# Delta-rule mixer: the identity added while evicting, projection products in threes, the last gate's products tied to the scan

## The chip, the cores and the metric

The kernel runs on one core of a Trainium2 chip. Its time is device time in microseconds, from one launch to its end; the time before is the median of three runs. The engines are TensorE (PE in the profile, with its weight loads as PEld), VectorE (DVE), ScalarE (ACT), GpSimd (POOL, idle here) and SyncE (SP), which issues the transfers. Each engine works through its own instructions in the order in which they were built.

## The reference, cut to what matters

Two network blocks run one after the other on 256 tokens of width 1024. The second holds, as its first mixer, a gated delta rule with 8 heads of 128 channels. Per head the tokens (256 of context and 256 of the sequence, in both directions) are cut into chunks, a triangular system is solved in each chunk, and a state is carried from chunk to chunk:

```python
lower = jnp.where(strict, jnp.einsum('nhcid,nhcjd->nhcij', kb, k) * decay, 0.0)
uw = lax.linalg.triangular_solve(lower, rhs, left_side=True, lower=True, unit_diagonal=True)
...
v_new = u_c - jnp.einsum('nhik,nhkv->nhiv', w_c, state)
o = jnp.einsum('nhik,nhkv->nhiv', qg_c, state) + jnp.einsum('nhij,nhjv->nhiv', qk_c, v_new)
state = state * a_c[..., None, None] + jnp.einsum('nhjk,nhjv->nhkv', kd_c, v_new)
```

q, k, v and a gate z come from projections of the modulated tokens; the outputs of the heads are normalised, gated by silu(z) and projected back.

## The kernel before

**Products.** A projection runs at fp32 accuracy as three products of split operands: with a high and a low part of each, `mm3` adds high by high (L172), low by high (L173) and high by low (L174) into one PSUM bank. One projection of 128 output channels on 512 tokens has 8 slices of the inner dimension and so 24 products of 128x512; in the trace they are `proj<-xh,whi`, `proj<-xl,whi` and `proj<-xh,wlo`. A head needs four such projections: q, k and v (through `dn_conv`, with a convolution over five taps, L964 and the lines next to it, on VectorE) and the gate z, at the end of `dn_scan`. The weights come by DMA in 512 KB pieces and are split on ScalarE (`whi`) and VectorE (`wlo`).

**The inverse.** `dn_inverse` inverts the triangular matrices of one head. There are two units, one per direction, each of four 128x128 matrices. Five levels are worked through, two units each, so a head has 10 steps and the stage 80. With the inverse x so far, its transpose xt and the level's mask m, a step is: `pw` = four f16 products of m and xt; w = pw copied to f16 by ScalarE (L1016); `pt` = identity times xt, one 128x512 product (L991), and four products of x and w added onto it; the new xt copied from `pt` by ScalarE (L1020); `px` = four products of w and x; the new x = x + px, added by VectorE (L1024). The tiles `dn_pw`, `dn_pt`, `dn_px` and `dn_pr` share two PSUM banks (tag `inv`). Each step of the one unit begins when a bank is free, and so the 10 steps follow each other: `dn_pw` starts a step, and the next `dn_pw` waits for the eviction of `dn_pt`. A closing part after the ten steps (64-wide products, a transpose, one refinement with fp32 products `dn_pr`, L1052 and L1055) gives the fp32 inverse `dn_xf`.

**The scan.** `dn_scan` carries the state through four chunks in two directions with fp32 products of 128x128 (`dn_st`, `dn_ob`, L1152 to L1171) and small evictions, then takes the gate's projection, normalises and writes y. After the last head the out-projection starts, with the same three products per slice; its tiles are named `proj` and `dn_pr`.

**What sets the order.** The code is written in the order solve(0), then for each head solve(head+1) and scan(head). A scheduler of the framework builds each engine's instruction list from this: among the instructions that it takes to be ready it places the one with the lowest priority number, which by default counts up in the order of the code. So the products of a later projection stand between the products of a step as filler: one, two or three of them while TensorE waits for w or for xt. `issue_after` is a means of that framework that holds instructions behind a named one, if it is on the same engine.

Of the kernel before, what the change touches and what calls it, by code (L numbers as in the profile page):

```python
# [14 lines left out]
AF = mybir.ActivationFunctionType  # L15
ALU = mybir.AluOpType
# [5 lines left out]
KD = D // P  # L22
S = 256
F = 2816
KF = F // P
EPS = 1e-6
WARM = 16


# [74 lines left out]
class Kernel:  # L104
# [60 lines left out]
            los.append(lo)  # L165
        return Split(his, n, shape), Split(los, n, shape)

    def mm3(self, out, pairs, first=True, last=True):

        n = len(pairs)  # L170
        for i, ((ah, al), (bh, bl)) in enumerate(pairs):
            self.nc.tensor.matmul(out, ah, bh, start=first and i == 0, stop=False)  # L172
            self.nc.tensor.matmul(out, ah, bl, start=False, stop=False)  # L173
            self.nc.tensor.matmul(out, al, bh, start=False, stop=last and i == n - 1)  # L174


    def rsqrt(self, out, x, shape, tag=""):
# [690 lines left out]

        self.nc.tensor.transpose(out, col.to_broadcast((P, P)), self.ident)

    def project2(self, w, j, x, name="proj2"):

        wh, wl = self.weight(w[j])
        m = wh.shape[2]
        flat = lambda t: t.rearrange("p s t -> p (s t)")
        ps = self.ch.psum([P, 2, S], name)
        self.mm3(flat(ps[:m]), [((wh[:, k], wl[:, k]), (flat(x[0][:, k]), flat(x[1][:, k]))) for k in range(KD)])
        return ps

    def project_apart(self, jobs, x, between=lambda: None):  # L880
# [94 lines left out]
    def dn_inverse(self, units):  # L975
# [3 lines left out]
        V, G = nc.vector, nc.scalar  # L979
        i16 = self.ident16.unsqueeze(1).to_broadcast((P, 4, P))  # L980
# [8 lines left out]
        def each(out, lhs, rhs, more=None):  # L989
            if more is not None:  # L990
                nc.tensor.matmul(out, self.ident16, more, start=True, stop=True)  # L991
            for c in range(4):
                nc.tensor.matmul(out[:, c], lhs[:, c], rhs[:, c], start=more is None, stop=True, skip_group_check=more is not None)  # L993
# [9 lines left out]
        xs, xts = [], []  # L1003
# [5 lines left out]
        for lv in range(1, 6):  # L1009
            ms = [off(n, lv) for n in range(2)]  # L1010
            for n in range(2):
                x, xt = xs[n], xts[n]
                pw = ch.psum([P, 4, P], "dn_pw")
                each(pw, ms[n], xt)
                w = new("dn_wm", 2)
                G.activation(w, pw, AF.Copy)  # L1016
                pt = ch.psum([P, 4, P], "dn_pt")
                each(pt, x, w, xt)
                xts[n] = new("dn_xt")
                G.activation(xts[n], pt, AF.Copy)  # L1020
                px = ch.psum([P, 4, P], "dn_px")
                each(px, w, x)
                xs[n] = new("dn_x")
                V.tensor_tensor(xs[n], x, px, op=ALU.add)  # L1024

        ws = []
        for n in range(2):
# [104 lines left out]
    def dn_scan(self, h, x, gt, parts, y):  # L1132
# [10 lines left out]
        for n in range(4):  # L1143
            if n % 2 == 0:
                ob = ch.psum([P, 2, P], "dn_ob")
            for d in range(2):
                s, c = st[d], n ^ d
                ps = ch.psum([P, 4, P], "dn_st")
                if s is None:
                    rhs = vt[:, c]  # L1150
                else:
                    nc.tensor.matmul(ps[:, 0], k[:, c], s, start=True, stop=True)  # L1152
                    rhs = ch.loc([P, P], "dn_rr", bufs=2)
                    V.scalar_tensor_tensor(rhs, ps[:, 0], at("neg", d, c), vt[:, c], op0=ALU.mult, op1=ALU.add)
                nc.tensor.matmul(ps[:, 1], xi[d][:, c], rhs, start=True, stop=True)
                if n < 3:
                    vk = ch.loc([P, P], "dn_vk", bufs=2)
                    G.activation(vk, ps[:, 1], AF.Copy, scale=at("bk", d, c))
                vn = ch.loc([P, P], "dn_vn", bufs=2)
                G.activation(vn, ps[:, 1], AF.Copy, scale=at("beta", d, c))  # L1160
                if n < 3:
                    nc.tensor.matmul(ps[:, 3], kt[:, c], vk, start=True, stop=True)
                    s2 = ch.loc([P, P], "dn_s", bufs=4)
                    if s is None:
                        V.tensor_copy(s2, ps[:, 3])
                    else:
                        V.scalar_tensor_tensor(s2, s, at("ge", d, c), ps[:, 3], op0=ALU.mult, op1=ALU.add)
                    st[d] = s2
                if s is not None:
                    nc.tensor.matmul(ps[:, 2], q[:, c], s, start=True, stop=True)  # L1170
                nc.tensor.matmul(ob[:, c % 2], dms[d][:, c], vn, start=n % 2 == 0 and d == 0, stop=n % 2 == 1, skip_group_check=True)  # L1171
                if n in (1, 2):
                    G.activation(o[:, c], ps[:, 2], AF.Copy, scale=at("eg", d, c))
                elif n == 3:
                    V.scalar_tensor_tensor(o[:, c], ps[:, 2], at("eg", d, c), o[:, c], op0=ALU.mult, op1=ALU.add)
            if n % 2:
                V.tensor_tensor(o[:, n - 1:n + 1], o[:, n - 1:n + 1], ob, op=ALU.add)
        pz = self.project2(self.A["dn_w"], 24 + h, x)
        z = ch.loc([P, 2, S], "dn_z", bufs=2)
        G.activation(z, pz, AF.Tanh, scale=0.5)  # L1180
        V.scalar_tensor_tensor(z, z, 1.0, pz, op0=ALU.add, op1=ALU.mult)
# [496 lines left out]
```

## Time and profile before

| | |
|---|---|
| time, median of three runs | 3092.65 us (3091.64 to 3095.69) |
| the profiled execution, its own time | 3096.87 us |
| its span, first to last instruction | 3095.1 us |
| mean granted TensorE clock | 0.987 of full speed (2.4 GHz) |
| TensorE busy | 3028.9 us, 98% |
| VectorE busy | 2383.8 us, 77% |
| ScalarE busy | 1846.0 us, 60% |
| delta-rule stage with the 80 steps, first to last `dn_pw` | 1557.84 to 1921.83 us |

The page gives the busy time of each engine over the span, then the span in 40 slices, the transfers, the chain of work that ended last, and the costliest groups. A matmul row's duration (0.39 us for most) is its latency; TensorE starts the next one before it ends, so what an instruction costs TensorE is the distance from its start to the next start. A busy TensorE can therefore still hold small waits.

### The profile page before, as it was taken

To read this page: it belongs to the slowest core of one execution; us is meant where nothing else is said; L and a number is where in the kernel's file an instruction comes from. 1 tells how busy PE (TensorE), PEld (TensorE's weight loads), DVE (VectorE), ACT (ScalarE), POOL (GpSimd) and SP (SyncE) were. 2 spreads that over 40 slices of the span, in tenths; PEclk is the share of its full clock that TensorE was granted. 3 is DMA by queue.
4 is the path that set the end of the run, shared out by engine and by line. 5 is a ranking of instruction groups with operands and counts; after the bars stand their busy time and mean duration, and the time that the engine had idled before them with its cause. 6 is when DMAs were issued, how large, how long until landed. Compare 5 with 4: busy or idle time off the path is not lost.

```text
span 3095.1 us, 53671 instructions
## 1 busy us (share of the span) xinstructions
PE 3028.9 (98%) x19974; PEld 2672.8 (86%) x19974; DVE 2383.8 (77%) x5017; ACT 1846.0 (60%) x3803; POOL 0.2 (0%) x4
## 2 busy tenths in 40 slices
PE   9999999999999999999999999999999999998999
PEld 9998999999899988888777777888888888896999
DVE  7888887888878878777888888677776766677766
ACT  5656566556665656666587777456554555556555
POOL 0000000000000000000000000000000000000000
PEclk9999999999999999999999999999999999998999
DMA  7653565566356635555211111244553444440455
GB/s 241 217 167 98 177 202 178 175 193 211 105 160 189 206 120 170 163 176 172 88 39 36 42 48 35 96 147 157 161 174 110 138 143 146 143 131 34 137 180 169
DMA packets 129861, 438.90 MB, mean 142 GB/s; under 512 B 14528, under 2 KB 18368, under 8 KB 129088
## 3 DMA queue, kind: packets, MB, share of 16 engines
q1 hardware_dynamic: 129456, 435.22, 44.3%
q8 instruction: 157, 2.57, 0.3%
q14 instruction: 104, 0.85, 0.1%
q10 hardware_dynamic: 144, 0.26, 0.0%
HBM read 433.32 MB, written 1.05 MB: 140 GB/s over the span
## 4 chain that ended last, share of the span: by engine, by line
PE 89%; DVE 5%; ACT 3%; DMA 1%; issue 1%; SPq 0%; ACTq 0%; DVEq 0%
PE gu L173 15%; PE gu L172 15%; PE gu L174 15%; PE dn L174 7%; PE dn L172 7%; PE dn L173 7%; PE proj L172 4%; PE proj L173 4%; PE proj L174 4%; DVE wlo L147 1%; ACT whi L146 1%; PE dn_pw L993 1%; PE dn_px L993 1%; PE dn_pt L993 1%; PE swa_pt L1347 1%
## 5 line engine op out<-in xcount | busy, mean ns | idle before, releaser
L146 ACT ACTIVATE whi<-raw 128x512 fp32r<-128x512 f32 (+1 forms) x1398 | 835.9, 604 | 860.4 <-PE gu L173 427.1
L147 DVE TENSOR_TENSOR wlo<-raw,whi 128x512 fp32r<-128x512 f32 (+1 forms) x1398 | 907.6, 657 | 407.7 <-ACT whi L146 393.8
L172 PE MATMUL gu<-xh,whi 128*128 128x256 f32 (+1 forms) x2800 | 907.3, 324 | 8.2 <-ACT xh L316 2.2
L173 PE MATMUL gu<-xl,whi 128*128 128x256 f32 (+1 forms) x2800 | 906.7, 324 | 0.9 <-DVE xl L325 0.7
L174 PE MATMUL gu<-xh,wlo 128*128 128x256 f32 (+1 forms) x2800 | 905.2, 324 | 0.2 <-DVE wlo L147 0.2
L172 PEld LDWEIGHTS gu<-xh,whi 128*128 128x128 f32 x2800 | 531.1, 190 | 54.2 <-ACT xh L324 4.4
L173 PEld LDWEIGHTS gu<-xl,whi 128*128 128x128 f32 x2800 | 530.9, 190 | 46.6 <-DVE xl L325 1.7
L174 PEld LDWEIGHTS gu<-xh,wlo 128*128 128x128 f32 x2800 | 530.4, 190 | 45.0 <-DVE wlo L147 0.4
L172 PE MATMUL dn<-hh,whi 128*128 128x256 f32 (+1 forms) x1388 | 447.4, 324 | 0.8
L174 PE MATMUL dn<-hh,wlo 128*128 128x256 f32 (+1 forms) x1388 | 446.5, 323 | 1.2 <-DVE wlo L147 1.2
L173 PE MATMUL dn<-hl,whi 128*128 128x256 f32 (+1 forms) x1388 | 446.0, 322 | 0.0
L172 PE MATMUL proj<-xh,whi 128*128 128x256 f32 (+2 forms) x936 | 307.6, 331 | 11.5 <-ACT lora_raw L542 4.0
L174 PE MATMUL proj<-xh,wlo 128*128 128x256 f32 (+2 forms) x936 | 307.1, 330 | 4.1 <-DVE wlo L147 4.1
L173 PE MATMUL proj<-xl,whi 128*128 128x256 f32 (+2 forms) x936 | 307.9, 331 | 2.1 <-DVE xl L317 1.9
L172 PEld LDWEIGHTS dn<-hh,whi 128*128 128x128 f32 x1388 | 263.1, 190 | 27.3 <-ACT hh L146 4.5
L174 PEld LDWEIGHTS dn<-hh,wlo 128*128 128x128 f32 x1388 | 262.7, 190 | 25.2 <-DVE wlo L147 3.9
L173 PEld LDWEIGHTS dn<-hl,whi 128*128 128x128 f32 x1388 | 263.4, 190 | 23.9 <-DVE hl L147 2.4
L172 PEld LDWEIGHTS proj<-xh,whi 128*128 128x128 f32 (+1 forms) x936 | 177.3, 190 | 22.0 <-ACT lora_raw L542 4.2
L174 PEld LDWEIGHTS proj<-xh,wlo 128*128 128x128 f32 (+1 forms) x936 | 177.9, 190 | 13.6 <-DVE wlo L147 4.9
L173 PEld LDWEIGHTS proj<-xl,whi 128*128 128x128 f32 (+1 forms) x936 | 177.8, 190 | 11.3 <-DVE xl L317 3.3
L461 DVE TENSOR_TENSOR ada_t<-ada_w,ada_c 128x1024 f32<-128x1024 f32 x144 | 175.4, 1218 | 6.2 <-DMA ada_w<-in_ada_w 6.2
L461 DVE TENSOR_TENSOR ada_w<-ada_w,ada_c 128x1024 f32<-128x1024 f32 x144 | 175.4, 1218 | 0.6
(522 smaller groups left out, 4016.6 us busy)
## 6 DMA issues: line engine op xcount, KB each, us to landing
raw<-in_ffn_gate SPq DMA_DIRECT2D x176, 512.0 KB, 3.8
raw<-in_ffn_up SPq DMA_DIRECT2D x176, 512.0 KB, 3.6
ada_w<-in_ada_w SPq DMA_DIRECT2D x144, 512.0 KB, 3.8
raw<-in_ffn_down SPq DMA_DIRECT2D x80, 448.0 KB, 3.4
raw<-in_ffn_down SPq DMA_DIRECT2D x40, 512.0 KB, 4.0
raw<-in_ffn_down SPq DMA_DIRECT2D x48, 384.0 KB, 3.2
raw<-in_dn_w SPq DMA_DIRECT2D x32, 512.0 KB, 3.4
raw<-in_ffn_down SPq DMA_DIRECT2D x48, 320.0 KB, 3.0
```

Source lines behind the costliest of these rows:

```text
L146: self.nc.scalar.activation(hi, src, AF.Copy)
L147: return self.nc.vector.tensor_tensor(lo, src, hi.bitcast(F32), op=ALU.subtract)
L172: self.nc.tensor.matmul(out, ah, bh, start=first and i == 0, stop=False)
L173: self.nc.tensor.matmul(out, ah, bl, start=False, stop=False)
L174: self.nc.tensor.matmul(out, al, bh, start=False, stop=last and i == n - 1)
L461: V.tensor_tensor(p, w, c[:, s], op=ALU.mult)
L993: nc.tensor.matmul(out[:, c], lhs[:, c], rhs[:, c], start=more is None, stop=True, skip_group_check=more is not None)
L1347: self.pinned(nc.tensor.transpose(pt[:, k], p[:, k // 2, (k % 2) * P:(k % 2 + 1) * P], self.ident))
```

## The change

Three things are changed.

1. In a step of the inverse, the eviction of `pw` goes from ScalarE to VectorE and adds the identity: w' = pw + I. Since x w' = x w + x, in either product, the transposed inverse is then `pt` = x w' without the product of the identity and xt, and the new x is `px` = w' x without the addition. The eviction of `px` goes from VectorE to ScalarE as a plain copy. 80 products of 128x512 go; the number of evictions stays.
2. `mm3` gets a switch `together`. With it, the second and third product of a slice get a priority number a million lower, so that the scheduler places them right behind the first. `project2` (q, k, v and z of each head, and not the out-projection, which calls `mm3` itself) sets it, except for the gate of head 7.
3. The gate of head 7 is wrapped in `issue_after(begun.ins)`, where `begun` is the ScalarE activation that writes `vn` in the first chunk of the last scan. That is an instruction of ScalarE, the products are TensorE's, and the lists that are built are the same with this line and without it. In them the 24 products of head 7's gate stand within head 6's inverse; before, they stand between head 6's inverse and head 7's.

```diff
+URGENT = 1_000_000
...
-    def mm3(self, out, pairs, first=True, last=True):
+    def mm3(self, out, pairs, first=True, last=True, together=False):
...
             self.nc.tensor.matmul(out, ah, bh, start=first and i == 0, stop=False)
+            self.tc.cur_priority -= URGENT * together
             self.nc.tensor.matmul(out, ah, bl, start=False, stop=False)
             self.nc.tensor.matmul(out, al, bh, start=False, stop=last and i == n - 1)
+            self.tc.cur_priority += URGENT * together
...
-    def project2(self, w, j, x, name="proj2"):
+    def project2(self, w, j, x, name="proj2", after=None):
...
-        self.mm3(flat(ps[:m]), [((wh[:, k], wl[:, k]), (flat(x[0][:, k]), flat(x[1][:, k]))) for k in range(KD)])
+        with self.tc.issue_after(after) if after else nullcontext():
+            self.mm3(flat(ps[:m]), [((wh[:, k], wl[:, k]), (flat(x[0][:, k]), flat(x[1][:, k]))) for k in range(KD)], together=not after)
...
                 w = new("dn_wm", 2)
-                G.activation(w, pw, AF.Copy)
+                V.tensor_tensor(w, pw, i16, op=ALU.add)
                 pt = ch.psum([P, 4, P], "dn_pt")
-                each(pt, x, w, xt)
+                each(pt, x, w)
...
                 each(px, w, x)
                 xs[n] = new("dn_x")
-                V.tensor_tensor(xs[n], x, px, op=ALU.add)
+                G.activation(xs[n], px, AF.Copy)
...
-                G.activation(vn, ps[:, 1], AF.Copy, scale=at("beta", d, c))
+                act = G.activation(vn, ps[:, 1], AF.Copy, scale=at("beta", d, c))
+                if n == 0:
+                    begun = act
...
-        pz = self.project2(self.A["dn_w"], 24 + h, x)
+        pz = self.project2(self.A["dn_w"], 24 + h, x, after=begun.ins if h == 7 else None)
```

The lists that are built show where the instructions stand. In the changed kernel L993 is L998, L1016 and L1024 are L1022 (on VectorE) and a copy on ScalarE, L172 to L174 are L174, L176 and L177, L1152 to L1171 are L1158 to L1179.

TensorE, inside a step of head 4's inverse, before: the four products of `dn_pw` end, and the next group of the step is `dn_pt`; the `proj` rows are a later projection, L1162 and L1171 the scan of the head before.

```order
L993 LDWEIGHTS dn_m_21747
L993 MATMUL dn_pw<-dn_xt,dn_m_21747 128x128
L173 MATMUL proj_22723<-xl,whi 128x512
L991 LDWEIGHTS ident_98
L991 MATMUL dn_pt<-dn_xt,ident_98 128x512
L1162 MATMUL dn_st<-dn_vk,dn_kt 128x128
L1171 MATMUL dn_ob<-dn_vn,dn_d 128x128
L993 LDWEIGHTS dn_x
L993 MATMUL dn_pt<-dn_wm,dn_x 128x128
```

The same engine and part of the program in the changed kernel, again from the end of `dn_pw` to the first product of `dn_pt`; L1089 is the transpose of the next head's k:

```order
L998 MATMUL dn_pw<-dn_xt,dn_m_21611 128x128
L1170 MATMUL dn_st<-dn_vk,dn_kt 128x128
L1179 MATMUL dn_ob<-dn_vn,dn_d 128x128
L1089 MATMUL dn_kr<-ident,dn_cv 128x128 x3
L1170 MATMUL dn_st<-dn_vk,dn_kt 128x128
L1179 MATMUL dn_ob<-dn_vn,dn_d 128x128
L1089 MATMUL dn_kr<-ident,dn_cv 128x128
L174 MATMUL proj_22948<-xh,whi 128x512
L176 MATMUL proj_22948<-xl,whi 128x512
L177 MATMUL proj_22948<-xh,wlo 128x512
L998 LDWEIGHTS dn_x
L998 MATMUL dn_pt<-dn_wm,dn_x 128x128
```

The product of the identity is gone, and the three products of a slice stand in one row where single ones stood.

VectorE in steps of the same head, before; L986 makes the mask of a level, L964 and L967 belong to a convolution, L147 to a weight's low part:

```order
L967 SCALAR_TENSOR_TENSOR dn_q<-dn_xp,dn_q 128x512
L147 TENSOR_TENSOR wlo<-raw,whi 128x512
L1024 TENSOR_TENSOR dn_x<-dn_x,dn_px 128x512
L986 TENSOR_TENSOR dn_m_21749<-dn_u_21625,lvl 128x512
L1154 SCALAR_TENSOR_TENSOR dn_rr<-dn_st,dn_neg,dn_vt 128x128 x2
L1078 TENSOR_SCALAR dn_m<-dn_ss 128x4
L964 SCALAR_TENSOR_TENSOR dn_cv<-dn_xp,small,dn_cv 128x512
L1024 TENSOR_TENSOR dn_x<-dn_x,dn_px 128x512
```

And in the changed kernel (L148 is the low part of a weight, L969 the convolution):

```order
L1022 TENSOR_TENSOR dn_wm<-dn_pw,ident_98 128x512
L991 TENSOR_TENSOR dn_m_21705<-dn_u_21585,lvl 128x512
L1160 SCALAR_TENSOR_TENSOR dn_rr<-dn_st,dn_neg,dn_vt 128x128 x2
L969 SCALAR_TENSOR_TENSOR dn_cv<-dn_xp,small,dn_cv 128x512
L148 TENSOR_TENSOR wlo<-raw,whi 128x512
L969 SCALAR_TENSOR_TENSOR dn_cv<-dn_xp,small,dn_cv 128x512
L1022 TENSOR_TENSOR dn_wm<-dn_pw,ident_98 128x512
```

Where the addition to x stood, the making of w stands now, behind the same convolutions and splits.

TensorE in the sixth step of head 7's inverse, before (`proj_24698` is the out-projection's first tile) and then in the changed kernel:

```order
L993 MATMUL dn_pw<-dn_xt,dn_m_23996 128x128
L1155 MATMUL dn_st<-dn_rr,dn_xf 128x128
L991 LDWEIGHTS ident_98
L991 MATMUL dn_pt<-dn_xt,ident_98 128x512
L174 MATMUL proj_24698<-xh,wlo 128x512
L172 MATMUL proj_24698<-xh,whi 128x512
L993 LDWEIGHTS dn_x
L993 MATMUL dn_pt<-dn_wm,dn_x 128x128
```

```order
L998 MATMUL dn_pw<-dn_xt,dn_m_23922 128x128
L1178 MATMUL dn_st<-dn_s,dn_q 128x128
L1161 MATMUL dn_st<-dn_rr,dn_xf 128x128
L1158 MATMUL dn_st<-dn_s,dn_k 128x128
L998 LDWEIGHTS dn_x
L998 MATMUL dn_pt<-dn_wm,dn_x 128x128
```

No projection product is left in that step.

## Rows read from the trace of the kernel before

**Rows 1.** The page, busy time, share of the span and instructions by engine.
```profile
PE 3028.9 (98%) x19974; PEld 2672.8 (86%) x19974; DVE 2383.8 (77%) x5017; ACT 1846.0 (60%) x3803; POOL 0.2 (0%) x4
```

**Rows 2.** Busy time by stretch: head 7's inverse, and the sum of all eight inverses.
```profile
core 0: us, PE busy (x) PEld busy (x) DVE busy (x) ACT busy (x) POOL busy (x), PEclk, DMA share, GB/s
...
1899.80:1921.80 22.00, 21.72 (x203) 17.57 (x200) 19.87 (x45) 19.49 (x49) 0.00 (x0) 1.00 0.08 26
...
sum 181.86, PE 180.83 PEld 145.21 DVE 155.20 ACT 148.99 POOL 0.00; mean PE 22.60 PEld 18.15 DVE 19.40 ACT 18.62 POOL 0.00
```

**Rows 3.** The same view of the seven stretches between the inverses: one, and their sum.
```profile
1767.20:1796.30 29.10, 29.10 (x189) 22.16 (x188) 25.13 (x70) 19.51 (x51) 0.00 (x0) 1.00 0.11 37
...
sum 182.10, PE 182.10 PEld 138.81 DVE 154.87 ACT 123.88 POOL 0.00; mean PE 26.01 PEld 19.83 DVE 22.12 ACT 17.70 POOL 0.00
```

**Rows 4.** The chain that ended last, from 1557.8 to 1921.9 us, by line.
```profile
by line: PE proj L172 13.6%; PE proj L173 13.5%; PE proj L174 13.2%; PE dn_pw L993 6.2%; PE dn_px L993 5.5%; PE dn_pt L993 5.1%; PE dn_pt L991 4.6%; PE dn_pr L993 3.7%; PE dn_st L1155 3.6%; PE dn_ob L1171 3.4%; PE dn_st L1170 3.4%; PE dn_st
```

**Rows 5.** Groups by line, 1557.8 to 1921.9 us: busy us, mean ns | idle before, releaser.
```profile
L991 PE MATMUL dn_pt<-dn_xt,ident 128*128 128x512 f16 x79 | 30.3, 384 | 0.0
...
L1016 ACT ACTIVATE dn_wm<-dn_pw 128x512 f16<-128x512 f32 x79 | 47.3, 599 | 11.1 <-PE dn_pw L993 9.9 <-PE dn_st L1170 0.8
...
L1024 DVE TENSOR_TENSOR dn_x<-dn_x,dn_px 128x512 f16<-128x512 f16 x79 | 54.1, 684 | 11.7 <-PE dn_px L993 11.1
...
L964 DVE SCALAR_TENSOR_TENSOR dn_cv<-dn_xp,small,dn_cv 128x512 f32<-128x512 f32 x52 | 38.8, 746 | 1.8 <-ACT dn_cv L962 1.8
```

**Rows 6.** TensorE in order of time, start and duration in us: from a step to the next.
```profile
1920.86 0.39 PE L993 MATMUL dn_px<-dn_x,dn_wm 128*128 128x128 f16 x4
1921.06 0.48 PE L174 MATMUL proj<-xh,wlo 128*128 128x512 f32 x1
1921.37 0.39 PE L172 MATMUL proj<-xh,whi 128*128 128x512 f32 x1
1921.60 0.39 PE L173 MATMUL proj<-xl,whi 128*128 128x512 f32 x1
1921.83 0.40 PE L993 MATMUL dn_pw<-dn_xt,dn_m 128*128 128x128 f16 x4
```

**Rows 7.** The same view, TensorE and ScalarE through one step of head 7.
```profile
1909.81 0.38 PE L993 MATMUL dn_pw<-dn_xt,dn_m 128*128 128x128 f16 x4
...
1910.29 0.60 ACT L1016 ACTIVATE dn_wm<-dn_pw 128x512 f16<-128x512 f32 x1
...
1910.86 0.39 PE L991 MATMUL dn_pt<-dn_xt,ident 128*128 128x512 f16 x1
...
1911.09 0.39 PE L993 MATMUL dn_pt<-dn_wm,dn_x 128*128 128x128 f16 x4
...
1911.51 0.60 ACT L1020 ACTIVATE dn_xt<-dn_pt 128x512 f16<-128x512 f32 x1 [0.37 <-PE dn_pt L993]
...
1912.16 0.38 PE L993 MATMUL dn_pw<-dn_xt,dn_m 128*128 128x128 f16 x4
```

**Rows 8.** The same view behind head 7's inverse; VectorE evicts `dn_pr` here.
```profile
1931.10 1.05 PE L993 MATMUL dn_pr<-dn_xf,dn_u 128*128 128x128 f32 x8
...
1931.99 0.39 PE L1155 MATMUL dn_st<-dn_vt,dn_xf 128*128 128x128 f32 x2
...
1932.13 0.48 PE L174 MATMUL proj<-xh,wlo 128*128 128x512 f32 x1
1932.19 0.69 DVE L1052 TENSOR_TENSOR dn_wm<-ident,dn_pr 128x512 f16<-128x512 f16 x1 [0.42 <-PE dn_pr L993]
...
1932.45 0.39 PE L172 MATMUL proj<-xh,whi 128*128 128x512 f32 x1
...
1932.94 0.40 PE L993 MATMUL dn_px<-dn_x,dn_wm 128*128 128x128 f16 x4
```

**Rows 9.** The same view: fp32 products of the scan in a row.
```profile
1906.96 0.39 PE L1162 MATMUL dn_st<-dn_vk,dn_kt 128*128 128x128 f32 x2
1907.19 0.39 PE L1171 MATMUL dn_ob<-dn_vn,dn_d 128*128 128x128 f32 x2
```

## The prediction

> **What bounds the kernel now.** I read the page first: TensorE is busy for 98% of the span [rows 1], so almost any wait that another engine causes shows as time, and so does any product that goes. Then the stretches. In the eight inverses TensorE is busy 180.83 of 181.86 us, VectorE 155.20, ScalarE 148.99 [rows 2]; between them it is 182.10 of 182.10, with VectorE at 154.87 [rows 3]. The granted clock is 1.00 in these stretches, so 2.4 GHz; nothing is lost to it. The chain of waits over the same 364 us runs along projection products (13.6, 13.5 and 13.2%), then the inverse's own [rows 4]. All of this looks like a stage bound by TensorE with VectorE 85% busy behind it.
>
> A busy TensorE still hides small waits here, since a row's 0.39 us is a latency. The distance from start to start gives the true cost: 0.23 us for a projection product (1921.37 to 1921.60), 0.20 to 0.22 for four f16 products [rows 6, 7], 0.23 for an fp32 pair [rows 9]; by the same distance the identity product takes 0.23 (1910.86 to 1911.09) [rows 7]. Counting the built order from the first `dn_pw` to the last with such costs gives 353 us of TensorE's work in the 364.0 us that passed. So about 11 us are waits. Where they are, a step shows: pw to w's eviction 0.48, to the next product 0.80, to xt's eviction 0.42, to the next pw 0.65, together 2.35 [rows 7]. The 0.80 holds the identity product; with TensorE ready as soon as w is, it would be the 0.65 seen behind xt, and the step 2.20. I take 2.30 for the chain of a step before. By my count 43 of 63 steps in heads 0 to 6 (each step counted up to the next, nine a head) and 7 of 9 in head 7 hold less TensorE work than that, and lack 6.5 and 1.8 us.
>
> **The change, part by part.** Everything is set against the profiled execution, 3096.87 us; it lies 4.2 above the median of the runs, 3092.65, so I carry differences over to the median.
>
> *The identity products.* 80 go. The chain of waits gives its line 4.6% of 364.1 us, 16.7 us for 79 products, 0.21 each [rows 4, 5]. Taken all as gain: 80 x 0.21 = **-17.0**. Ends: where the step waits on its chain the product was filler and gives nothing, which the terms on the chain below take back; all at 0.23 [rows 7] it would be -18.4.
>
> *Products in threes.* The same products stand in fewer blocks: 173 instead of 231 in this window. A first product behind f16 products starts the next one 0.31 later, not 0.23, while the f16 set in front of it took 0.20 for 0.22: about 0.06 for such a switch [rows 6]. Behind an fp32 pair the two distances, 0.14 and 0.32, add up to 0.46, as much as 0.23 and 0.23 [rows 8, 9]: nothing, or some 0.01. The blocks that go stood behind the identity (55 to 14) and behind fp32 products (98 to 79); those behind f16 products stay (78 to 80). So **-0.7**, with ends 0 and 58 x 0.06 = -3.5.
>
> On this one the Trainium skill ("TensorE: Matmul & The Clock Gate", section "Part 2: What happens when you issue a matmul") says that the next product's weights are loaded while the current matmul runs, which would make a switch free; the term would be 0 and the forecast 3087.0. The 0.31 in rows 6 speaks against it for f16 neighbours.
>
> *The chain of a step.* w is now made by VectorE: 684 ns in place of 599 for such an eviction [rows 5], so the chain goes from 2.30 to about 2.40. VectorE as evictor shows 0.75 from its start at 1932.19 to the next product at 1932.94 [rows 8], against 0.65 behind ScalarE [rows 7]: the same 0.1. px's eviction goes the other way, but the next use of x comes a step later, under it lies the other unit's step. Against this, fillers move in: in heads 0 to 6 the steps hold more products (297 in all steps, before 167), and only 18 of 63 are short of 2.40, by 3.7 us together. **-2.8** (3.7 - 6.5). Their ends: 2.8 us short at a chain of 2.35, 7.0 at 2.55, so -3.7 and +0.5.
>
> *Head 7's inverse loses its fillers.* The products in threes come earlier, the last gate's with them: its 24 products stand in head 6's inverse and the out-projection's first ones behind that. The hold-back names a ScalarE instruction and so moves nothing on TensorE. No projection product is left in the nine steps of head 7; their TensorE work falls from 19.6 to 12.8 us, while nine chains of 2.40 are 21.6. Waits 8.8 instead of 1.8: **+7.0**. With a chain of 2.20 it is 7.0 - 1.8 = +5.2; with 2.55, +8.4. The head took 22.00 us before [rows 2], so in effect this part stays as long as it was although its identity products go.
>
> *The part behind head 7's inverse.* The 21 products that stand earlier in all are worth 21 x 0.23 = 4.9 us; they lengthen the window and should shorten what is behind it. From the last pw at 1921.83 [rows 6] to the first scan product at 1931.99 [rows 8] are 10.2 us with 26 of them; 6 stay. But there is a chain there as well: about nine links of a product and an eviction, 0.42 + 0.63 each [rows 7], 9.4 us. So it shortens by 0.8 only, **+4.1** (0 to +4.9).
>
> *VectorE's queue.* Its load hardly changes (an addition leaves, an addition comes), but w now stands in its order behind convolution steps of 0.75 us [rows 5] and weight splits, and TensorE waits for w, then xt, then the next step. Counted per step with such durations, 33 of 72 steps hold more than 2.4 us of VectorE's own work (10 before); what goes beyond the step's chain and TensorE's work adds up to 4.1 us (1.1 before): **+3.0**. Ends: 0, if w is always first; the upper end is the first rival.
>
> SyncE's list and the order of the transfers are the same, and the scan and the normalisation behind head 7's `dn_xf` stay as they are.
>
> Sum: -17.0 - 0.7 - 2.8 + 7.0 + 4.1 + 3.0 = **-6.4 us**. The profiled execution would be 3090.5, the median 3092.65 - 6.4 = **3086.2**.
>
> **Rivals.** *VectorE's queue takes over, slower.* One mechanism: w waits behind a whole further instruction of VectorE, 0.75 us [rows 5], in n of the 72 steps. For it: VectorE is busy for 85% of the inverses [rows 2], and it sat idle for only 11.7 us before the 79 additions of L1024, 0.15 each [rows 5], so it mostly comes to such an instruction straight from another. Against it: TensorE's filler in the same step hides part of a wait. Without my +3.0 the sum is -9.4; -9.4 + 0.75 n passes +6.2 from n = 21. With a third of the steps, n = 24, it is +8.6: 3101. The Trainium skill ("TensorE: Matmul & The Clock Gate", section "Architectural detail: the array is 16× 32×32, not 1× 128×128") states that VectorE's queue is strictly first in, first out, which is what this rival needs; the traced rows don't decide how often it bites.
>
> *No change.* The same mechanism with n near 12, or a chain of 2.55 to 2.60 in all steps: what the identity gives is spent in waits. -9.4 + 9.0 = -0.4, so about 3092. For it: the three engines are within 20% of each other in the inverses [rows 2], and the window's waits were already 11 us.
>
> *More gain.* VectorE never late for w, the chain 2.20, every block that goes worth 0.06: -17.0 - 3.5 - 2.8 + 5.2 + 4.1 = -14.0, 3078.6. For it: TensorE busy for 180.83 of 181.86 [rows 2].
>
> *The change doesn't do what it says.* For the hold-back that is certain from the built order and is in the forecast; had it kept the gate's products for head 7, some +7.0 + 4.1 of the sum would go, and the time would be near 3076.
>
> **How the numbers follow.** A measurement of this kernel tells about 0.2%, 6.2 us, from no change; the forecast lies just beyond that. Chances: the forecast and its neighbourhood (-3 to -11) 0.50, more gain (beyond -11) 0.13, no change (-3 to +6) 0.26, slower 0.11. Of the forecast's 0.50 a good two thirds lie beyond -6.2 (0.37): faster 0.37 + 0.13 = 0.50; same 0.13 + 0.26 = 0.39; slower 0.11. The range goes from the gain of the third rival, 3078, to 3096, +3.4, halfway from no change to slower; the forecast's own is 3081.5 to 3089.5.
>
> **What would show it.** In the changed profile: no `dn_pt<-dn_xt,ident` row; the stretch from first to last `dn_pw` near 358 us, not 364; steps of heads 1 to 6 near 2.4 us or longer where threes stand in them; head 7's nine steps still about 21.5 us with TensorE well under 22 busy and ScalarE and VectorE as releasers; 9 to 10 us from the last `dn_pw` to the scan. VectorE as releaser of `dn_pt` with idle time of more than 10 us over the stage would speak for the first rival. I am wrong on the mechanism if the stretch shortens by 14 or more, if it doesn't shorten, or if head 7 gets shorter by over 2 us.

## The result and the profile after

The changed kernel takes 3120.95 us (median; 3115.59 to 3123.58) against 3094.17 us of the kernel before beside it: a ratio of 1.0083, 95% interval 1.0063 to 1.0102. It is slower by 26.8 us, where 6.4 us less were forecast. The profiled execution is the shortest of the four, 3115.59 us.

The page of the changed kernel, the span and the row that answers to [rows 1]:

```profile
span 3113.6 us, 53527 instructions
...
PE 3020.1 (97%) x19894; PEld 2669.8 (86%) x19894; DVE 2383.2 (77%) x5017; ACT 1844.5 (59%) x3803; POOL 0.2 (0%) x4
```

80 instructions fewer and 8.8 us less busy time on TensorE, but 18.5 us more span. The loss lies in the forecast's own window: from the first `dn_pw` to the last are 385.4 us (1555.94 to 1941.34), not 364.0. The busy time by stretch, as in [rows 2]: the inverses of heads 6 and 7 and the sum of all eight (columns: us; busy us and count of PE, PEld, DVE, ACT, POOL; granted clock; DMA share; GB/s).

```profile
core 0: us, PE busy (x) PEld busy (x) DVE busy (x) ACT busy (x) POOL busy (x), PEclk, DMA share, GB/s
...
1867.73:1896.91 29.18, 28.81 (x225) 23.78 (x222) 23.94 (x57) 22.40 (x63) 0.00 (x0) 0.88 0.01 1
1919.19:1941.34 22.15, 17.86 (x172) 14.43 (x170) 15.79 (x46) 15.82 (x43) 0.00 (x0) 0.97 0.00 1
sum 208.04, PE 201.51 PEld 163.65 DVE 165.66 ACT 156.66 POOL 0.00; mean PE 25.19 PEld 20.46 DVE 20.71 ACT 19.58 POOL 0.00
```

And the stretches between the inverses, as in [rows 3], the one from head 4 to head 5 and the sum of the seven:

```profile
1784.45:1814.40 29.95, 25.95 (x169) 20.07 (x169) 22.80 (x69) 18.65 (x49) 0.00 (x0) 0.93 0.15 53
...
sum 177.36, PE 161.03 PEld 124.17 DVE 146.59 ACT 115.21 POOL 0.00; mean PE 23.00 PEld 17.74 DVE 20.94 ACT 16.46 POOL 0.00
```

Set against the forecast, part by part (us; the forecast of a part is its time before, plus what the terms put there; for the first and the third line it is an estimate, since the prediction gives only their sum with the second, some 358 us):

| part | before | forecast | measured |
|---|---|---|---|
| inverses of heads 0 to 6 | 159.9 | 176 to 179 | 185.9 |
| inverse of head 7 | 22.0 | 22.2 | 22.15 |
| seven stretches between | 182.1 | 157 to 160 | 177.4 |
| last `dn_pw` to the scan | 10.2 | 9.4 | 11.2 |

The third line holds most of the error. 109 projection products, 25 us, left these stretches; the time fell by 4.7. Before, TensorE was busy for all 182.10 us of them [rows 3]; now it is idle for 16.3 of 177.36. In the inverses it is idle for 6.5 of 208.04 us, 4.3 of them in head 7 (1.0 of 181.86 before, [rows 2]). The view of what TensorE waited for, over the whole stage (waiting line, releaser: us in total, times, longest), shows who it waits for. The first line of the fence is all that this view has of the kernel before, the next ones are the longest in the changed kernel.

```profile
engine line waited for: us in total, times, longest us
PE dn_pt L993 <- ACT dn_wm L1016: 0.2, 1, 0.2
...
PE dn_st L1161 <- ACT dn_vt L1070: 3.5, 4, 1.3
PE dn_pt L998 <- DVE dn_wm L1022: 3.3, 5, 1.1
PE dn_tr L1069 <- ACT dn_d L1128: 2.4, 4, 1.5
PE dn_pk L1106 <- ACT dn_k L1070: 2.1, 3, 0.8
```

`dn_tr`, `dn_pk` and `dn_st` belong to the next head's set-up and the scan. The wait for w, my first rival, has 3.3 us in five places, not the 24 waits that it needed; four of the five (2.2 us) are in head 7's inverse.

The granted clock is the second new thing. TensorE in order of time at the end of the set-up of head 5 (start, duration, line; in brackets the idle time and its releaser):

```profile
1805.79 0.38 PE L1123 MATMUL dn_pg<-dn_rows,dn_pick 128*128 128x512 bf16 x1
1807.71 0.38 PE L1122 MATMUL dn_pg<-tri,identb 128*128 128x512 bf16 x1 [1.55 <-ACT dn_d L1128]
1807.93 0.38 PE L1123 MATMUL dn_pg<-dn_rows,dn_pick 128*128 128x512 bf16 x1
1809.81 0.73 PE L1069 MATMUL dn_tr<-ident,dn_cv 128*128 128x128 f32 x4 [1.50 <-ACT dn_d L1128]
...
1811.43 1.23 PE L1161 MATMUL dn_st<-dn_vt,dn_xf 128*128 128x128 f32 x4 [0.20 <-ACT dn_vt L1070]
1812.45 1.71 PE L978 MATMUL dn_ss<-ones,dn_sq 128*128 128x1 f32 x8
```

and the same place by stretches of 4 us (the granted clock is the third number from the right):

```profile
1804.00:1808.00 4.00, 2.45 (x13) 1.41 (x12) 1.77 (x5) 2.74 (x7) 0.00 (x0) 1.00 0.26 105
1808.00:1812.00 4.00, 2.21 (x12) 1.33 (x11) 3.97 (x12) 3.26 (x8) 0.00 (x0) 0.78 0.00 0
1812.00:1816.00 4.00, 4.00 (x25) 4.00 (x24) 2.11 (x6) 2.31 (x6) 0.00 (x0) 0.50 0.01 2
1816.00:1820.00 4.00, 4.00 (x37) 3.49 (x36) 2.81 (x10) 1.34 (x3) 0.00 (x0) 0.86 0.00 0
```

Two waits of 1.5 us with little work between them, and the clock falls from 1.00 to 0.50, 2.4 to 1.2 GHz, just as the next head's inverse starts. This happens at five places, each behind such waits, none of them longer than 1.55 us. Over 1540 to 1980 us such rows lack 13.7 us of full clock in all, an upper bound of its price; before, no row lacks any. The same stretch in one row, before and then changed:

```profile
1540.00:1980.00 440.00, 435.70 (x3283) 343.09 (x3282) 365.26 (x943) 313.77 (x768) 0.00 (x0) 1.00 0.15 50
...
1540.00:1980.00 440.00, 411.96 (x3077) 326.98 (x3076) 346.57 (x896) 300.14 (x744) 0.00 (x0) 0.97 0.12 39
```

The low clock also reaches the inverses: the granted clock is 0.94, 0.95 and 0.88 in those of heads 3, 5 and 6, so they lack 6.4 us of full clock. With the 2.2 us of idle time there, that is about the 7 to 10 us by which the first line of the table is longer than forecast.

### The profile page after: what moved, and what is told of

Read it like the earlier page. It is cut to its first block, busy times and chain, and to the rows that moved or that the text cites. A ratio compares the mean times of both kernels' runs of the same rounds, so it can differ in the third digit from the quotient of the medians.

```text
span 3113.6 us, 53527 instructions
## 1 busy us (share of the span) xinstructions
PE 3020.1 (97%) x19894; PEld 2669.8 (86%) x19894; DVE 2383.2 (77%) x5017; ACT 1844.5 (59%) x3803; POOL 0.2 (0%) x4
## 4 chain that ended last, share of the span: by engine, by line
PE 87%; DVE 6%; ACT 4%; DMA 1%; issue 1%; SPq 0%; ACTq 0%; DVEq 0%
PE gu L174 15%; PE gu L176 15%; PE gu L177 15%; PE dn L177 6%; PE dn L174 6%; PE dn L176 6%; PE proj L174 4%; PE proj L176 4%; PE proj L177 3%; DVE wlo L148 1%; ACT whi L147 1%; DMA raw<-in_ffn_down 1%; PE dn_pw L998 1%; PE dn_pt L998 1%; PE swa_o L1401 1%
## 5 line engine op out<-in xcount | busy, mean ns | idle before, releaser
L147 ACT ACTIVATE whi<-raw 128x512 fp32r<-128x512 f32 (+1 forms) x1398 | 835.5, 604 | 853.0 <-PE gu L176 425.4
L148 DVE TENSOR_TENSOR wlo<-raw,whi 128x512 fp32r<-128x512 f32 (+1 forms) x1398 | 908.5, 658 | 415.4 <-ACT whi L147 397.3
L174 PE MATMUL gu<-xh,whi 128*128 128x256 f32 (+1 forms) x2800 | 906.5, 324 | 9.4 <-ACT xh L328 3.0
L176 PE MATMUL gu<-xl,whi 128*128 128x256 f32 (+1 forms) x2800 | 905.9, 324 | 1.3 <-DVE xl L329 1.1
L177 PE MATMUL gu<-xh,wlo 128*128 128x256 f32 (+1 forms) x2800 | 904.8, 324 | 0.0
L174 PEld LDWEIGHTS gu<-xh,whi 128*128 128x128 f32 x2800 | 530.4, 190 | 55.6 <-ACT xh L328 5.4
L176 PEld LDWEIGHTS gu<-xl,whi 128*128 128x128 f32 x2800 | 530.1, 189 | 46.9 <-DVE xl L329 2.3
L177 PEld LDWEIGHTS gu<-xh,wlo 128*128 128x128 f32 x2800 | 529.7, 189 | 44.6 <-DVE wlo L148 0.3
L174 PE MATMUL dn<-hh,whi 128*128 128x256 f32 (+1 forms) x1388 | 447.6, 324 | 0.7
L177 PE MATMUL dn<-hh,wlo 128*128 128x256 f32 (+1 forms) x1388 | 446.7, 323 | 1.6 <-DVE wlo L148 1.6
L176 PE MATMUL dn<-hl,whi 128*128 128x256 f32 (+1 forms) x1388 | 446.3, 323 | 0.0
L174 PE MATMUL proj<-xh,whi 128*128 128x256 f32 (+2 forms) x936 | 315.5, 340 | 14.3 <-ACT lora_raw L546 4.1
L176 PE MATMUL proj<-xl,whi 128*128 128x256 f32 (+2 forms) x936 | 300.6, 323 | 2.4 <-DVE xl L321 1.7
L177 PE MATMUL proj<-xh,wlo 128*128 128x256 f32 (+2 forms) x936 | 299.3, 322 | 3.2 <-DVE wlo L148 3.2
L174 PEld LDWEIGHTS dn<-hh,whi 128*128 128x128 f32 x1388 | 263.3, 190 | 27.1 <-ACT hh L147 4.5
L177 PEld LDWEIGHTS dn<-hh,wlo 128*128 128x128 f32 x1388 | 262.9, 190 | 25.4 <-DVE wlo L148 4.5
L176 PEld LDWEIGHTS dn<-hl,whi 128*128 128x128 f32 x1388 | 263.5, 190 | 23.9 <-DVE hl L148 2.4
L174 PEld LDWEIGHTS proj<-xh,whi 128*128 128x128 f32 (+1 forms) x936 | 177.9, 191 | 25.1 <-issue 7.5
L177 PEld LDWEIGHTS proj<-xh,wlo 128*128 128x128 f32 (+1 forms) x936 | 178.2, 191 | 16.0 <-DVE wlo L148 3.8
L176 PEld LDWEIGHTS proj<-xl,whi 128*128 128x128 f32 (+1 forms) x936 | 178.4, 191 | 10.6 <-DVE xl L321 3.5
```

What stands on the lines that cost most here:

```text
L147: self.nc.scalar.activation(hi, src, AF.Copy)
L148: return self.nc.vector.tensor_tensor(lo, src, hi.bitcast(F32), op=ALU.subtract)
```

## Experiments

The first four take the change apart into the identity, the threes and the hold-back. Theory A at the start: the threes use up early the products that filled the wait for the next head's set-up. Theory B, the rival: w on VectorE lengthens every step. Theories C (a loop of waits) and D (the clock) come from what the fourth showed.

**The identity alone**: of the diff only the lines of `dn_inverse`.

```diff
-                G.activation(w, pw, AF.Copy)
+                V.tensor_tensor(w, pw, i16, op=ALU.add)
...
-                each(pt, x, w, xt)
+                each(pt, x, w)
...
-                V.tensor_tensor(xs[n], x, px, op=ALU.add)
+                G.activation(xs[n], px, AF.Copy)
```

> Only the identity's part of the change: w' = pw + I evicted by VectorE, px copied by ScalarE, no identity product; the projection products stay in their old order rule (no threes, no hold-back). In its built list 24 to 28 projection products stand behind dn_pq of the next head (25 in the kernel before; 6 to 24 in the changed one), and 31 in head 7's inverse (0 in the changed one). Theory A (the threes use up the products that fill the wait for the next head's set-up): this kernel keeps the filler and gains what the identity costs, about 3085 us, stretches between the inverses with some 1 us of TensorE idle each. Theory B (w on VectorE lengthens every step): the loss of the changed kernel is here too, 3105 to 3121 us.

Measured: 3082.01 us, ratio 0.9950 (0.9936 to 0.9964). The two sums, inverses and stretches between:

```profile
sum 194.30, PE 192.77 PEld 156.77 DVE 173.01 ACT 157.19 POOL 0.00; mean PE 24.10 PEld 19.60 DVE 21.63 ACT 19.65 POOL 0.00
...
sum 155.40, PE 155.17 PEld 119.39 DVE 137.96 ACT 115.09 POOL 0.00; mean PE 22.17 PEld 17.06 DVE 19.71 ACT 16.44 POOL 0.00
```

TensorE is without idle time between the inverses again, the window is 349.7 us, and w on VectorE does no visible harm. The identity's part is a gain; theory B falls.

**The threes alone**: the changed kernel with `dn_inverse` as before (the diff above, reversed).

> Only the threes (and the hold-back line), with the identity products, w on ScalarE and the addition to x on VectorE as before. In its list 18 products stand behind dn_pq of heads 2 to 6, 0 behind that of head 7, and none in head 7's inverse. Theory A: slower than before although no work is added, 3100 to 3115 us, with the waits between the inverses and in head 7. Theory B: about as before, 3090 to 3097 us.

Measured: 3124.28 us, ratio 1.0085 (1.0071 to 1.0098), beyond what I expected of them. The whole loss is theirs. The stretch between heads 6 and 7 and the sum of the seven:

```profile
1896.90:1924.50 27.60, 22.91 (x153) 16.78 (x153) 21.40 (x63) 15.70 (x44) 0.00 (x0) 0.95 0.13 39
sum 193.40, PE 178.22 PEld 136.58 DVE 159.44 ACT 124.11 POOL 0.00; mean PE 25.46 PEld 19.51 DVE 22.78 ACT 17.73 POOL 0.00
```

15.2 us of idle time, with no product taken away. So in the changed kernel the identity's gain didn't get lost on the way: its TensorE time was taken out of a kernel in which TensorE waits (388.4 us of window with the threes alone, 385.4 with both).

**The hold-back made to work**: the last gate behind a TensorE product.

```diff
-                nc.tensor.matmul(ps[:, 1], xi[d][:, c], rhs, start=True, stop=True)
+                first = nc.tensor.matmul(ps[:, 1], xi[d][:, c], rhs, start=True, stop=True)
+                if n == 0:
+                    begun = first
...
-                act = G.activation(vn, ps[:, 1], AF.Copy, scale=at("beta", d, c))
-                if n == 0:
-                    begun = act
+                G.activation(vn, ps[:, 1], AF.Copy, scale=at("beta", d, c))
```

> The changed kernel with the last gate held behind a TensorE product of the last scan instead of a ScalarE activation. In its list no projection product stands in head 6's inverse from then on, between 6 and 7, and in head 7's inverse; 60 more stand behind it. Theory A: another 24 + products of filler leave the inverses, so slower still than the changed kernel, 3125 to 3140 us. Theory B: as the changed kernel, 3116 to 3124 us. My prediction had put this case near 3076 us.

Measured: 3123.76 us, ratio 1.0092 (1.0076 to 1.0109), not to be told from the changed kernel, and far from the 3076 of my fourth rival. But the held products go behind head 7's inverse, not into it, so the rival's own case, products kept for head 7, isn't tested here; that they leave head 6 as well cost less than theory A had it.

**Filler put back behind the set-up**: every gate held behind `dn_pq` of the next head.

```diff
-        pz = self.project2(self.A["dn_w"], 24 + h, x, after=begun.ins if h == 7 else None)
+        pz = self.project2(self.A["dn_w"], 24 + h, x, after=self.held_by.ins)
```

(`held_by` is the last product of `dn_pq`, and the gates go by threes.)

> The changed kernel with the gate's products of every head held behind dn_pq of the next head (for head 7 its own), by threes too. In its list 27 products stand behind dn_pq of each head and 51 in head 7's inverse. Theory A: the waits between the inverses and in head 7 go, some 20 + 7 us, so 3080 to 3095 us, while the steps stay as long as in the changed kernel. Theory B: the steps stay long and with them the time, 3110 to 3121 us.

Measured: 3157.47 us, ratio 1.0196 (1.0182 to 1.0209). Neither of my two cases has this time. Theory A falls in its simple form. The sum of the stretches between and the first row of TensorE's waits:

```profile
sum 217.80, PE 167.75 PEld 128.47 DVE 148.75 ACT 111.66 POOL 0.00; mean PE 23.96 PEld 18.35 DVE 21.25 ACT 15.95 POOL 0.00
...
PE dn_kp L1069 <- DVE dn_m L1195: 23.9, 5, 4.8
```

Filler stands behind `dn_pq` as I wanted, and these stretches hold 50 us of idle time, all of it ahead of `dn_pq` or within it; the longest wait by far is that of the set-up's `dn_kp` for L1195. (The clock falls behind these waits too: six of the seven stretches have a granted clock of 0.84 or 0.85.) That is the normalisation at the end of the scan of the head before. Why should a head's set-up wait for it?

**The loop.** Followed through the changed kernel, one turn reads (start, duration, engine; rows of TensorE, VectorE and ScalarE, from head 3's scan to head 5's inverse):

```profile
1759.60 0.27 PE L1089 MATMUL dn_kr<-ident,dn_cv 128*128 128x128 f32 x1
...
1783.48 0.41 DVE L1185 TENSOR_TENSOR dn_o<-dn_o,dn_ob 128x256 f32<-128x256 f32 x1
...
1785.13 0.31 ACT L1193 ACTIVATE dn_os<-dn_o 128x128 f32<-128x128 f32 x1
...
1785.57 0.28 ACT L1092 ACTIVATE dn_os<-dn_kr 128x128 f32<-128x128 f32 x1
...
1792.46 0.16 DVE L1200 SCALAR_TENSOR_TENSOR dn_r<-dn_r,dn_r 128x4 f32<-128x4 f32 x1
...
1793.27 0.16 DVE L185 TENSOR_SCALAR dn_r<-dn_m 128x8 int32<-128x8 int32 x1
...
1797.82 0.69 DVE L1099 TENSOR_TENSOR dn_kt<-dn_kr,dn_r 128x512 f32<-128x512 f32 x1
...
1798.60 0.69 DVE L1061 TENSOR_TENSOR dn_xf<-dn_x,dn_px 128x512 f32<-128x512 f16 x1
...
1814.40 0.63 PE L998 MATMUL dn_pw<-dn_xt,dn_m 128*128 128x128 f16 x4
```

Head 5's k stands in PSUM from 1759.60 on, but its squares (L1092) use the one buffer of `dn_os`, which the scan's squares (L1193) hold until 1785.5. Its scaling `dn_r` (two buffers) is written only behind L1200, the last use of head 3's. Then `dn_kt`, and 16.6 us of set-up until the first `dn_pw`, at whose end the next scan starts: head 4's inverse `dn_xf` is there at 1799.3, but the scan's first product stands at 1811.43 (in the rows above), behind `dn_tr`, which stood behind the set-up's `dn_pg` and waited for its eviction. So scan, normalisation and set-up follow one another. From the six turns of heads 1 to 6 I take the means: last scan squares behind the head's first `dn_pw`, from there to `dn_kt`, and from there to the next head's first `dn_pw`.

| | last squares | to `dn_kt` | to `dn_pw` | period |
|---|---|---|---|---|
| before | 23.6 | 13.5 | 14.0 | 51.0 |
| identity alone | 22.8 | 10.3 | 14.8 | 47.9 |
| changed | 25.2 | 13.2 | 15.1 | 53.5 |
| threes alone | 25.2 | 15.2 | 14.5 | 54.9 |

Against the identity alone the threes lengthen the first two pieces by 2.4 and 2.9 us or more. The pieces add up to the period by the way they are cut, so they don't tell how long the chain would be by itself; with the identity alone it fits into 47.9 us. Before, TensorE's own work fills the same turn. That is theory C, with theory D on the clock beside it.

**The loop opened**, in the changed kernel:

```diff
-            sq = ch.loc([P, P], "dn_os")
+            sq = ch.loc([P, P], "dn_ks")
             G.activation(sq, pt[:, c], AF.Square, accum_out=m[:, 4 + c:5 + c])
...
-        r = ch.loc([P, 8], "dn_r", bufs=2)
+        r = ch.loc([P, 8], "dn_r", bufs=3)
```

> The changed kernel (identity and threes) with a third buffer for dn_r and a tile of their own for the squares of k. In the changed kernel a head's period is a loop of waits: the scan ends 20 to 25 us after the head's first dn_pw, its last squares release the tile of the squares of k, 11 to 15 us later stands dn_kt of the next head, and 15 us later that head's first dn_pw. Theory C (the threes lengthen this loop, and TensorE idles because the loop, not its work, sets the period): with the loop opened dn_kt comes earlier and the time falls by 15 to 35 us against the changed kernel, to 3085 to 3106. Theory A (only the filler behind the set-up counts; 21 to 33 products stand behind dn_pq here, 6 to 24 in the changed kernel): also faster, but by no more than the 20 us of waits between the inverses. Theory of long steps alone: as the changed kernel, 3116 to 3124.

Measured: 3075.46 us, ratio 0.9935 (0.9923 to 0.9946); 45 us less than the changed kernel from two buffers. The same events, again head 5's set-up:

```profile
1747.63 0.39 PE L1089 MATMUL dn_kr<-ident,dn_cv 128*128 128x128 f32 x2
...
1748.58 0.29 ACT L1092 ACTIVATE dn_ks<-dn_kr 128x128 f32<-128x128 f32 x1
...
1752.87 0.31 ACT L1193 ACTIVATE dn_os<-dn_o 128x128 f32<-128x128 f32 x1
...
1759.96 0.69 DVE L1099 TENSOR_TENSOR dn_kt<-dn_kr,dn_r 128x512 f32<-128x512 f32 x1
...
1778.99 0.39 PE L998 MATMUL dn_pw<-dn_xt,dn_m 128*128 128x128 f16 x4
```

k's squares follow its transposes after 1 us, ahead of the scan's. The stretches between, summed, have 0.3 us of idle time:

```profile
sum 130.10, PE 129.82 PEld 103.10 DVE 112.46 ACT 101.12 POOL 0.00; mean PE 18.55 PEld 14.73 DVE 16.07 ACT 14.45 POOL 0.00
```

The edit also moves products in the list: by the expectation 21 to 33 of them stand behind `dn_pq`, and 6 to 24 in the changed kernel. So this run alone doesn't part the loop from theory A; the third buffer alone, below, does.

**The identity alone with the loop opened** (the same two edits):

> The kernel with the identity's part alone, with the same third buffer for dn_r and own tile for the squares of k. There TensorE is idle for some 1 us per stretch between the inverses, so it is TensorE's work that sets the period: theory C expects little, 3074 to 3083 us, the same within 0.2% as the identity alone. If the loop set the period there too, 3060 to 3072.

Measured: 3072.69 us, ratio 0.9928 (0.9913 to 0.9942), the lowest of all. It lies between my two cases, 3074 to 3083 and 3060 to 3072. By the ratios it is some 7 us below the identity alone, with intervals that overlap; so theory C's "little" holds roughly, and a small share of the loop in that kernel can't be excluded. It beats both kernels.

**Pairs in place of threes**, in the changed kernel:

```diff
-            self.tc.cur_priority -= URGENT * together
             self.nc.tensor.matmul(out, ah, bl, start=False, stop=False)
+            self.tc.cur_priority -= URGENT * together
             self.nc.tensor.matmul(out, al, bh, start=False, stop=last and i == n - 1)
```

> The changed kernel with blocks of two: only the third product of a slice is tied to the second, the first stands free. In its list 37 to 41 products stand in the steps of a head, 9 to 21 behind dn_pq of the next head and none in head 7's inverse, much as in the changed kernel. If the size of a block is what delays the loop (at most one product of 0.23 us more in front of a ready instruction instead of two), about half of the loss against the identity alone is left: 3095 to 3108. If it is where the products stand (running ahead), as the changed kernel: 3114 to 3124.

Measured: 3106.03 us, ratio 1.0036 (1.0024 to 1.0048). A bit over half of the loss against the identity alone (24 of 39 us) is left, with a mean period of 51.9 us: the size of the blocks counts, though as many products run ahead.

**The idle time filled with useless work**, in the changed kernel:

```diff
+        def transposed(x, idle=0):
             pt = ch.psum([P, 4, P], "dn_pt", F16)
+            for c in range(idle):
+                nc.tensor.transpose(pt[:, c % 4], self.ident16, self.ident16)
...
-            xts.append(transposed(x))
+            xts.append(transposed(x, 24))
```

> The changed kernel with 24 more transposes of the identity (0.056 us each) ahead of each unit's first transpose, overwritten afterwards: 384 in all, 21.5 us of TensorE's time at full clock, standing around dn_pg of each next head, where the changed kernel waits. In the changed kernel's trace the granted clock is 0.5 to 0.86 in the 8 to 12 us behind such waits. Theory D (the waits lower TensorE's clock and this is a good part of the loss): faster than the changed kernel although work is added, by 3 to 10 us, and the granted clock is 1.00 there. Without an effect of the clock: slower by 5 to 21 us.

Measured: 3113.60 us, ratio 1.0061 (1.0049 to 1.0072), 7 us below the changed kernel's median with 21.5 us of work more; the two ratios' intervals still touch, so the size is uncertain. The trace is clearer: the window falls from 385.4 to 380.8 us, with 651 projection products in both and some 18.8 us of useless work put in; TensorE's idle time goes from 22.9 to 11.5 us, and the granted clock from 0.97 to 1.00 (the window in the changed kernel, then here):

```profile
1555.94:1941.34 385.40, 362.54 (x2785) 287.81 (x2783) 312.25 (x811) 271.87 (x675) 0.00 (x0) 0.97 0.12 39
...
1560.84:1941.64 380.80, 369.34 (x3113) 299.14 (x3118) 311.74 (x811) 272.29 (x675) 0.00 (x0) 1.00 0.13 40
```

Those 18.8 us (336 of the 384 transposes at 0.056 us) in place of 11.4 us of idle time would by themselves have made the window longer. The stretch that answers to the clock of 0.50 above, and the eight products of the same line, which took 1.71 us there:

```profile
1812.00:1816.00 4.00, 4.00 (x33) 3.23 (x34) 3.69 (x11) 2.11 (x6) 0.00 (x0) 1.00 0.01 2
...
1811.58 0.95 PE L978 MATMUL dn_ss<-ones,dn_sq 128*128 128x1 f32 x8
```

Theory D holds beside theory C: some of the loss is the clock that falls in the waits.

**The kernel before, and the threes alone, with the loop opened** (the two edits of buffers again):

> The kernel before with the third buffer for dn_r and the own tile for the squares of k, nothing else. Its waits between the inverses are about 1 us each, so its period is TensorE's work: theory C expects 3086 to 3096 us, little or no change. If the loop had been the limit there too, 3070 to 3082.

> The threes alone (identity products kept) with the same two edits. Theory C: with the loop opened the threes cost next to nothing, so about the kernel before with the loop opened, plus 0 to 6 us: 3088 to 3100, some 25 to 35 below the threes alone (3124). If the threes cost time by themselves (blocks in front of ready instructions in every step), 3108 to 3124.

Measured: 3096.31 us, ratio 1.0000 (0.9991 to 1.0010), and 3093.30 us, ratio 0.9989 (0.9980 to 0.9997). The loop doesn't set the time of the kernel before, and with it opened the threes cost nothing there. All eight combinations, as the window from the first `dn_pw` to the last in the traces:

| us | loop as it was | loop opened |
|---|---|---|
| before | 364.0 | 363.0 |
| threes | 388.4 | 360.4 |
| identity | 349.7 | 341.7 |
| both | 385.4 | 344.5 |

The windows don't hold the same work: from top to bottom 630, 651, 644 and 651 projection products lie in them with the loop as it was, and 631, 630, 621 and 643 with it opened; the others stand ahead or behind. At 0.23 us each [rows 6], up to 7 us of a difference can come from that.

**The third buffer alone**, in the changed kernel (the second line of the two edits):

> The changed kernel with the third buffer for dn_r alone; the squares of k stay in the tile that the scan's squares use. In its list dn_kt still stands behind the tenth step of the head before, as in the changed kernel, where it stands before the tenth step with both edits in some heads. If the shared tile closes the loop: as the changed kernel, 3112 to 3124. If the buffer of dn_r closes it: 3075 to 3095.

Measured: 3096.26 us, ratio 1.0000 (0.9991 to 1.0009), between my two cases: the buffer of `dn_r` is worth 25 us, the tile of the squares another 21. Both close the loop. Behind `dn_pq` of heads 2 to 7 stand 17 or 18 projection products here, 6 to 24 (17 in the mean) in the changed kernel: the 25 us came without putting filler back. But the period of 50.1 us is shorter mostly in its first piece (22.1 us, from 25.2) and hardly in the one to `dn_kt` (12.7, from 13.2), so how the third buffer shortens the turn is not shown.

**The identity taken out of the refinement too**, on top of the fastest:

```diff
-            each(pr, u, xf, xt)
+            each(pr, u, xf)
             r = new("dn_wm", 2)
-            V.tensor_tensor(r, i16, pr, op=ALU.subtract)
+            V.tensor_tensor(r, i16, xt, op=ALU.subtract)
+            V.tensor_tensor(r, r, pr, op=ALU.subtract)
```

> The identity's part with the loop opened, and the 16 identity products of the refinement (dn_pr) taken out as well: VectorE subtracts xt from the identity first (f16, about 0.42 us, 16 times) and then pr. A test of the price of an identity product: where TensorE's work sets the period, 16 x 0.21 = 3.4 us less, so a ratio to the kernel before of 0.9917 (0.9928 without this edit), 3066 to 3073 us. If such products stood in waits and cost nothing, or VectorE's 6.7 us more count, 0.993 to 0.995.

Measured: 3079.07 us, ratio 0.9944 (0.9930 to 0.9957): a miss for the price, and within the range of my other case. The window is 343.9 us, 2.2 longer than without the edit, but it holds 639 projection products and not 621, worth some 4.1 us. The rest of the span is 4.5 longer, at a mean granted clock of 0.986 over the span in place of 0.989. So the trace doesn't show a loss in the steps, and whether VectorE's 16 additional instructions eat the 3.4 us is not shown.

## Why the prediction was wrong

*The identity products* (-17.0) were sized right where TensorE's work sets the time: the window falls by 14.3 us with the identity alone, by 15.9 and 21.3 with the loop opened; set to equal counts of projection products, by an estimate of 17.5, 18.9 and 19.0. With threes and the closed loop it is 3.0. The price of an instruction holds only as long as its engine is the bound.

*The step that failed* is the one on the chain of a step: "fillers move in: in heads 0 to 6 the steps hold more products". I counted what they fill there and left the place they come from to TensorE's account, at 0.23 us each. I had no term for the stretches between the inverses, because TensorE was busy for 182.10 of 182.10 us there [rows 3], and I asked for no chain in them as I did for the step and for head 7. There was one, covered: it fitted into the 51.0 us of a head before. The scan, the normalisation and the set-up waited for each other through two buffers, and the threes both lengthened it and took its cover. The mis-forecast is the waits that came up, 16.3 us between the inverses and 2.2 in those of heads 0 to 6, and the lower clock behind them. An estimate of the window's 21.4 us more: -17.0 for the identity products, +4.8 for 21 projection products more, +21.9 for idle time (22.9, before 1.0), and at most +11 for full clock that lacks; together 20.7.

*The clock.* "Nothing is lost to it" was true of the trace of before and not of the change: idle time costs more than itself, when the clock falls behind it. The Trainium skill ("TensorE: Matmul & The Clock Gate", section "HAM oscillation — how this bites in real kernels") describes this for a kernel whose matmuls come in bursts with waits between them: the array falls back to its lower clock and the next burst runs at it. The trace agrees, with 0.50 behind the two waits; the waits here, 1.55 and 1.50 us, are on ScalarE, not on transfers.

*Products in threes* (-0.7): with the loop opened the window is 2.6 us shorter with the threes than without, and 2.8 longer where the identity products are gone; but there it holds 22 projection products more. At equal counts the estimates are -2.4 and -2.3, within the term's ends; the whole times don't tell them from nothing (3093.30 and 3096.31; 3075.46 and 3072.69).

*Head 7* (+7.0): right in its time, 22.15 us with 17.86 of TensorE busy (22.00 and 21.72 in [rows 2]). *Behind it* (+4.1): the chain was there, 11.2 us and not 9.4.

*VectorE's queue* (+3.0, and the slower rival at 3101): the sign of the result was the rival's, its mechanism wasn't. TensorE waited 3.3 us for w, 1.1 of them outside head 7, and the identity alone is faster. The second of the signs against me, a stretch that doesn't shorten, is what came.

What stays open: which instruction behind a block of three delays the loop most (TensorE's own scan products or VectorE's convolutions of heads further ahead), and how exactly the loss divides between waits and clock: the estimate above has the clock at its upper bound, and the filled idle time shows its part with an uncertain size.

## What to carry to other kernels

Before moving filler out of a stretch in which an engine is fully busy, look for the loop that the filler covers: follow one tile from one turn to the next and see which buffers make the turns wait. Blocks that are tied together delay whatever becomes ready behind them, so a larger block needs slack in that loop. Where a loop closes through a buffer and not through data, a buffer more can be worth more than the work saved.

## What the runs showed of the hardware

TensorE's granted clock fell from 1.00 to 0.50 behind two waits of 1.55 and 1.50 us with two products between them; eight 128x1 products took 1.71 us at the lower level and 0.95 at the higher. Useless products in such waits kept the clock at 1.00 there, and the stage ran 4.6 us shorter with them. And VectorE as the evictor that the step waits for, 0.09 us longer than ScalarE [rows 5], cost nothing that could be told: with the identity alone no wait of TensorE for w is listed.
